# The last branch of a hybrid encoder layer: gate products kept in the gates' tiles, accumulators swapped each chunk, A22 split and multiplied ahead of S4

## The chip, the cores and the metric

The kernel runs on one core of a Trainium2 chip. A core has five instruction streams that work side by side and meet at semaphores: TensorE (PE in the profile; its weight loads are PEld), VectorE (DVE), ScalarE (ACT), GpSimd (POOL) and SyncE (SP, which here only issues DMAs). Each stream executes its own instructions strictly in order. The metric is the device time of one execution in microseconds (us).

## The reference

One layer of an encoder is applied to two requests of 256 and 512 tokens, 768 in all, with the same weights. Cut to the part that the change touches:

```python
h = rmsnorm(x, norm_mix_g)
u, q, k, v, qm, gl = split(h @ w_in)
branches = stack([s5_out, diff_out, mem_out])           # three token mixers
br = einsum('blnc,ncd->blnd', branches, w_branch)       # each projected, 1024 -> 1024
gates = sigmoid(gl + b_gate)
merged = sum(gates * br, axis=branch)
x = x + merged @ w_out                                  # the output projection
h2 = rmsnorm(x, ffn_norm_g)
x = x + (silu(h2 @ w_gate) * (h2 @ w_up)) @ w_down
```

All arrays are float32.

## The kernel before, in words

Activations are kept transposed, features on the 128 partitions and the 768 tokens along the free axis. Every float32 operand of a matmul is held as two parts, hi (`wh`, written by ACT with a copy that rounds) and lo (`wl`, the difference, written by DVE), and a product is three matmuls: hi·hi, hi·lo, lo·hi. They are L755, L756 and L757 of the helper `mm3`, so all products of the kernel carry these three lines, and a profile is read by the tiles.

The branches are projected and merged one after the other: memory attention, S5, and last differential attention. The last one, `branch7`, is what the change touches. It runs in four chunks `c` of 256 output features. In a chunk, the 2x2 blocks of weights (A11 to A22, 512 x 128 each) and of activations (B11 to B22, 512 features x 384 tokens each) are multiplied by the Winograd scheme with seven block products in place of eight: A11·B11, A12·B21, S1·T1, S2·T2, S3·T3, S4·B22 and A22·T4. Each block product is twelve matmuls of 128 x 128 weights on 384 columns. S1 to S4 are sums of weight blocks, made by POOL (L574, L575, L581, L583) in tiles `ws`; S4 overwrites S2. T1 to T4 are sums of activation blocks.

`_split_w` makes a chunk's weights one chunk ahead. `_factor` splits one block into hi and lo (L557 on ACT, L558 on DVE); two blocks share one pair of tiles, so that seven blocks fill three and a half pairs and the last one shares with the next chunk's A11. Raw weights arrive by SP's DMAs in tiles `wr`.

The results of a chunk lie in two accumulator tiles `cs[0]` = (c11, c12) and `cs[1]` = (c21, c22), named `bs` in the profile and taken from a pool of two buffers. Three products (A11·B11, S2·T2, S3·T3) add up in one PSUM bank, `brc`, and are copied out by ACT in between (L1683, L1685, L1690); the others come in banks `br` and are added by DVE (L1673). The gates' logits come from DRAM by a DMA that POOL issues (L1657) into tiles `glr`, of which there are two buffers; ACT makes tanh of them (L1658). `merge(m)` then finishes half m of the chunk, a block M = 2c + m of 128 features: DVE forms (tanh + 1) x accumulator (L1677), the product is added to `merged` (L1678, on POOL for m = 0 and on DVE for m = 1), and `merged` is split into the hi and lo parts of `MG` (L1679 on ACT, L1680 on DVE; tile `mgd`), which are the operand of the output projection.

The output projection (`out_rows`, tiles `wo`) takes the eight blocks M of `MG` as its inner dimension; its weights are w_out, tiles `wr56` to `wr59`, split by L599 (ACT) and L605 (DVE). Its PSUM banks are given out anew when the branch's banks are closed.

A scheduler of the language fixes the order in which each engine's instructions stand, from the order in the code and its own estimate of when each becomes ready. It moves a product ahead of another where it holds it to be ready earlier. In tile names the first number counts the weight matrices in the stream: 52 to 55 are the four chunks of `branch7`, 56 and 57 the first two of w_out. A tile shared by two blocks bears the name of the first (`wl55_S1` holds S1 and S3).

## Time and profile before

| | us |
|---|---|
| three runs | 1741.29, 1742.41, 1743.65 (median 1742.41) |
| the profiled execution, its own time | 1743.06 |
| its span, first to last instruction | 1741.3 |
| PE busy in the span | 1726.6 |
| first matmul of the last branch starts (from the span's start) | 1120.74 |
| first matmul of the output projection starts | 1183.75 |

Times in the trace count from the start of the span. A row of the timeline gives start, duration, engine, line, operation, the tiles written and read, and in brackets how long the engine had been idle and whose work ended that. Durations of matmuls overlap their neighbours, since they are pipelined; the pace of PE is read from one start to the next.

### The profile page before, as it was taken

The numbers are of one execution on the slowest core, as the hardware profiler recorded it, in microseconds if no ns is written. First come the engines' busy times: TensorE is split into PE (matmuls) and PEld (weight loads), VectorE is DVE, ScalarE is ACT, GpSimd is POOL, SyncE is SP. The second block draws the span as 40 slices with busy tenths as digits, with TensorE's granted clock in tenths as the row PEclk, the third lists the DMA queues.
The fourth block names the chain that finished last, engine by engine and source line by source line (L and its number), as shares of the span: only waits on it lengthen the run. The fifth ranks groups of instructions, "written<-read, shape, count | busy, mean of one in ns | idle before, by whom it ended". The sixth has DMA issues, their size and how long they took to land.

```text
span 1741.3 us, 29531 instructions
## 1 busy us (share of the span) xinstructions
PE 1726.6 (99%) x11188; PEld 1608.1 (92%) x11188; DVE 1300.5 (75%) x2405; ACT 908.6 (52%) x1924; POOL 302.5 (17%) x308
## 2 busy tenths in 40 slices
PE   9999999999999999999999999999999999999999
PEld 9999988999999999999989888998889999998887
DVE  7665749699999778887886536685598777776775
ACT  7444543776767346877765434353343333334443
POOL 0000000000000100111000001341036555541130
PEclk9999999999999999999999999999999999999999
DMA  7222636755556454745653435335312323239974
GB/s 268 78 85 91 125 120 135 186 125 143 145 159 159 115 140 103 164 91 156 155 165 117 140 116 157 103 111 174 97 55 91 110 91 109 92 110 295 248 157 97
DMA packets 209213, 234.09 MB, mean 134 GB/s; under 512 B 57832, under 2 KB 173296, under 8 KB 209072
## 3 DMA queue, kind: packets, MB, share of 16 engines
q1 hardware_dynamic: 182160, 167.49, 32.0%
q0 software_dynamic: 17440, 58.34, 15.6%
q10 hardware_dynamic: 9472, 6.39, 1.3%
q8 instruction: 88, 1.44, 0.4%
q14 instruction: 53, 0.43, 0.1%
HBM read 165.78 MB, written 41.22 MB: 119 GB/s over the span
## 4 chain that ended last, share of the span: by engine, by line
PE 95%; DVE 2%; ACT 1%; issue 0%; DMA 0%; POOL 0%; SPq 0%; ACTq 0%; DVEq 0%
PE gl L755 4%; PE gl L756 4%; PE gl L757 4%; PE gate L755 3%; PE gate L756 3%; PE up L756 3%; PE gate L757 3%; PE up L755 3%; PE up L757 3%; PE dn L757 3%; PE dn L755 3%; PE dn L756 3%; PE br L755 3%; PE br L757 3%; PE br L756 3%; PE qk L755 3%
## 5 line engine op out<-in xcount | busy, mean ns | idle before, releaser
L599 ACT ACTIVATE wh<-wr 128x1024 fp32r<-128x1024 f32 x116 | 131.9, 1138 | 52.3 <-PE br L756 13.3
L605 DVE TENSOR_TENSOR wl<-wr,wh 128x1024 fp32r<-128x1024 f32 x74 | 99.2, 1342 | 63.5 <-ACT wh L599 61.7
L755 PE MATMUL gl<-H,wh 128*128 128x256 f32 (+1 forms) x384 | 132.2, 344 | 0.0
L757 PE MATMUL gl<-H,wl 128*128 128x256 f32 (+1 forms) x384 | 129.0, 336 | 0.0
L756 PE MATMUL gl<-H,wh 128*128 128x256 f32 (+1 forms) x384 | 128.7, 335 | 0.0
L603 POOL DMA_DIRECT2D wl<-wr x42 | 36.6, 872 | 483.3 <-ACT wl L602 464.1
L755 PE MATMUL qk<-wh,H 128*128 128x256 f32 x384 | 108.3, 282 | 0.0
L756 PE MATMUL qk<-wl,H 128*128 128x256 f32 x384 | 108.0, 281 | 0.0
L757 PE MATMUL qk<-wh,H 128*128 128x256 f32 x384 | 107.3, 279 | 0.0
L558 DVE TENSOR_TENSOR wl_S<-ws,wh_S 128x512 fp32r<-128x512 f32 x84 | 70.7, 863 | 26.2 <-ACT wh_S L557 26.2
L756 PE MATMUL dn<-wld,dxh 128*128 128x512 f32 x231 | 89.6, 389 | 0.0
L755 PE MATMUL dn<-whd,dxh 128*128 128x512 f32 x231 | 89.5, 389 | 0.0
L757 PE MATMUL dn<-whd,dxl 128*128 128x512 f32 x231 | 88.9, 389 | 0.0
L557 ACT ACTIVATE wh_S<-ws 128x512 fp32r<-128x512 f32 x84 | 49.5, 625 | 73.5 <-PE up L756 36.6
L757 PEld LDWEIGHTS gl<-H,wl 128*128 128x128 f32 x384 | 72.0, 188 | 8.1
L756 PEld LDWEIGHTS gl<-H,wh 128*128 128x128 f32 x384 | 72.2, 188 | 7.2
L755 PEld LDWEIGHTS gl<-H,wh 128*128 128x128 f32 x384 | 72.3, 188 | 6.9
L757 PEld LDWEIGHTS qk<-wh,H 128*128 128x128 f32 x384 | 72.6, 189 | 0.6
L755 PEld LDWEIGHTS qk<-wh,H 128*128 128x128 f32 x384 | 72.4, 188 | 0.6
L756 PEld LDWEIGHTS qk<-wl,H 128*128 128x128 f32 x384 | 72.3, 188 | 0.5
L1296 DVE TENSOR_REDUCE nm<-sc 128x1 f32<-128x512 f32 (+1 forms) x96 | 56.7, 597 | 18.1 <-PE sc L1291 17.2
L1298 ACT ACTIVATE p<-sc,nm 128x512 f32<-128x512 f32 (+1 forms) x96 | 58.8, 615 | 14.4 <-DVE nm L1296 13.9
(535 smaller groups left out, 6076.2 us busy)
## 6 DMA issues: line engine op xcount, KB each, us to landing
wr<-in_w_in_dram SPq DMA_DIRECT2D x48, 512.0 KB, 5.0
wr<-in_w_gate_up_dram SPq DMA_DIRECT2D x44, 512.0 KB, 3.6
wl<-wr POOLq DMA_DIRECT2D x42, 512.0 KB, 5.4
wr<-in_w_branch_dram SPq DMA_DIRECT2D x24, 512.0 KB, 4.5
glr<-gl_scr POOLq DMA_DIRECT2D x24, 384.0 KB, 3.5
hid_scr<-fa SPq DMA_DIRECT2D x11, 768.0 KB, 6.4
wr<-in_w_mem_kv_dram SPq DMA_DIRECT2D x16, 512.0 KB, 4.4
wr<-in_w_in_dram SPq DMA_DIRECT2D x32, 256.0 KB, 3.9
```

What stands on the lines that cost most here:

```text
L557: self.nc.scalar.activation(f(hi), src, AF.Copy)
L558: self.nc.vector.tensor_tensor(out=f(lo), in0=src, in1=f(hi).bitcast(F32), op=ALU.subtract)
L599: self.nc.scalar.activation(hi, r, AF.Copy)
L603: self.nc.gpsimd.dma_start(lo, r.bitcast(F32R), accum_op=ALU.add)
L605: self.sub.tensor_tensor(out=lo, in0=r, in1=hi.bitcast(F32), op=ALU.subtract)
L755: pe.matmul(ps, wh, xh, start=start, stop=False, **kw)
L756: pe.matmul(ps, wh, xl, start=False, stop=False, **kw)
L757: pe.matmul(ps, wl, xh, start=False, stop=stop, **kw)
L1296: v.tensor_reduce(out=nm[:, m : m + 1], in_=ps, axis=AX.X, op=ALU.max, negate=True)
L1298: act.activation(pm[:, 0:n], ps, AF.Exp, bias=nm[:, m : m + 1], accum_out=s1s[:, tt : tt + 1] if m == 0 else s2)
```

## The change

Five things are done, all in the last branch:

- the product of gate and accumulator is written into the gate's tile (`gs[m]`) and no longer into the accumulator, so that an accumulator is free after L1684 (L1677 before), and a gate's tile only after the add to `merged` (L1685);
- in odd chunks the two accumulator tiles change places (`cs.reverse()`);
- in every chunk, and not only in the last, A22·T4 and `merge(1)` stand before S4·B22 and `merge(0)`, and for these weights A22 is split before S4;
- S1·T1 stands before S2·T2;
- in the last chunk the add to `merged` of `merge(0)` is done by DVE, not by POOL.

```diff
-        self._factor(i, "S4", s4)
-        self._factor(i, "A22", A22)
+        for key, src in (("A22", A22), ("S4", s4)) if inplace else (("S4", s4), ("A22", A22)):
+            self._factor(i, key, src)
...
+        def merged_parts(M):
+            act.activation(MG[0][:, M], merged[:, M], AF.Copy, scale=0.5)
+            v.scalar_tensor_tensor(out=MG[1][:, M], in0=merged[:, M], scalar=0.5,
+                                   in1=MG[0][:, M].bitcast(F32), op0=mul, op1=sub)
...
+                if c % 2:
+                    cs.reverse()
...
-                    v.scalar_tensor_tensor(out=cs[m], in0=gs[m], scalar=1.0, in1=cs[m], op0=add, op1=mul)
-                    (v if m else gp).tensor_tensor(out=merged[:, M], in0=merged[:, M], in1=cs[m], op=add)
...
+                    v.scalar_tensor_tensor(out=gs[m], in0=gs[m], scalar=1.0, in1=cs[m], op0=add, op1=mul)
+                    (v if m or c == 3 else gp).tensor_tensor(out=merged[:, M], in0=merged[:, M], in1=gs[m], op=add)
+                    merged_parts(M)
 
                 act.activation(c11, prod("A11", "B11", chain), AF.Copy)
                 plus(c11, prod("A12", "B21"))
-                act.activation(c12, prod("S2", "T2", chain, False), AF.Copy)
                 p5 = prod("S1", "T1")
                 act.activation(c22, p5, AF.Copy)
+                act.activation(c12, prod("S2", "T2", chain, False), AF.Copy)
                 prod("S3", "T3", chain, False)
                 plus(c22, chain)
                 act.activation(c21, chain, AF.Copy)
...
+                plus(c21, prod("A22", "T4"))
+                merge(1)
+                plus(c12, prod("S4", "B22", p5, False))
+                merge(0)
```

What the scheduler makes of it is shown at three places.

**Place 1, the middle of chunk 2.** On PE, before, S1·T1 of chunk 2 (`br_1502`) is followed by the first product of chunk 3 (`brc_1508`), whose third matmul needs the lo part of chunk 3's A11, the second half of `wl54_A22_13775`:

```order
L757 MATMUL br_1502_13972<-rb_12988,wl54_S2_13760 128x384
L755 MATMUL brc_1508_14055<-ra_12987,wh54_A22_13774 128x384 [waits Activation_49]
L756 MATMUL brc_1508_14055<-ra_12987,wh54_A22_13774 128x384
L757 MATMUL brc_1508_14055<-ra_12987,wl54_A22_13775 128x384 [waits DVE_49]
L755 MATMUL brc_1508_14055<-ra_12987,wh54_A22_13774 128x384
```

Now only the two matmuls with the hi part stand there:

```order
L757 MATMUL br_1502_13959<-rb_12988,wl54_S2_13760 128x384
L755 MATMUL brc_1508_14055<-ra_12987,wh54_S4_13774 128x384 [waits Activation_49]
L756 MATMUL brc_1508_14055<-ra_12987,wh54_S4_13774 128x384
L755 MATMUL brc_1500_13931<-rc_12989,wh54_S2_13759 128x384 [waits Activation_49]
L756 MATMUL brc_1500_13931<-rc_12989,wh54_S2_13759 128x384
```

The first matmul with the lo part has moved behind 36 others: S2·T2, A22·T4 and S4·B22 of chunk 2. Three more of that product follow, and then S3·T3 of chunk 2, which waits for the copy of c12 out of the bank on ACT. That copy, with its neighbours on ACT, before:

```order
L1679 ACTIVATE mgd_13595<-merged_11575 128x768 [waits DVE_49]
L1687 ACTIVATE bs_1499_13930<-br_1502_13972 128x384 [waits PE_49]
L1658 ACTIVATE glr_1497_13926<-glr_1497_13926 128x768 [waits DMASW3_49,Activation_49]
L557 ACTIVATE wh55_S1_13906<-ws550_13896 128x512 [waits PE_49,Activation_49]
L1685 ACTIVATE bs_1498_13929<-brc_1500_13931 128x384 [waits PE_49]
```

and now:

```order
L1649 ACTIVATE mgd_13595<-merged_11575 128x768 [waits DVE_49]
L557 ACTIVATE wh55_S1_13906<-ws550_13896 128x512 [waits PE_49,Activation_49]
L1692 ACTIVATE bs_1498_13929<-brc_1500_13931 128x384 [waits PE_49]
L1663 ACTIVATE glr_1497_13926<-glr_1497_13926 128x768 [waits DMASW3_49,Activation_49]
L557 ACTIVATE wh55_S1_13906<-ws552_13910 128x512 [waits Pool_49]
```

The copy (L1685, now L1692) stands behind the hi part of block M = 3 of `merged` in both, and the tanh of the gate has gone behind it.

**Place 2, the end of chunk 2 on DVE.** The rows begin with the add to c22, and the gate's tile `glr_1497` is freed for the last gate (`glr_1505`) by L1677 before:

```order
L1673 TENSOR_TENSOR bs_1499_13930<-bs_1499_13930,brc_1500_13931 128x384 [waits PE_49]
L605 TENSOR_TENSOR wl56_0_14036<-wr56_0_13778,wh56_0_14035 128x1024 [waits DMAHW5_49,Activation_49]
L1673 TENSOR_TENSOR bs_1499_13930<-bs_1499_13930,br_1503_14017 128x384 [waits Activation_49]
L1680 SCALAR_TENSOR_TENSOR mgd_13595<-merged_11575,mgd_13595 128x768 [waits Activation_49]
L1673 TENSOR_TENSOR bs_1506_14053<-bs_1506_14053,br_1509_14069 128x384 [waits DVE_49,PE_49,Activation_49]
L1677 SCALAR_TENSOR_TENSOR bs_1499_13930<-glr_1497_13926,bs_1499_13930 128x768 [waits DVE_49]
```

and by L1685 now:

```order
L1680 TENSOR_TENSOR bs_1499_13930<-bs_1499_13930,brc_1500_13931 128x384 [waits PE_49]
L558 TENSOR_TENSOR wl55_A22_13916<-wr55_1_13747,wh55_A22_13915 128x512 [waits Activation_49]
L558 TENSOR_TENSOR wl55_A22_13916<-ws551_13897,wh55_A22_13915 128x512 [waits Activation_49]
L1680 TENSOR_TENSOR bs_1499_13930<-bs_1499_13930,br_1503_14000 128x384 [waits Activation_49]
L1684 SCALAR_TENSOR_TENSOR glr_1497_13926<-glr_1497_13926,bs_1499_13930 128x768 [waits DVE_49]
L605 TENSOR_TENSOR wl56_0_14036<-wr56_0_13778,wh56_0_14035 128x1024 [waits DMAHW5_49,PE_49,Activation_49]
L1680 TENSOR_TENSOR bs_1507_14054<-bs_1507_14054,br_1509_14069 128x384 [waits PE_49,Activation_49]
L1685 TENSOR_TENSOR merged_11575<-merged_11575,glr_1497_13926 128x768 [waits DVE_49]
```

The splits of A22 and S4 of chunk 3, which stood ahead of these rows, now stand among them.

**Place 3, from the branch to the output projection.** On PE the last block product was S4·B22 (`br_1510`):

```order
L757 MATMUL br_1510_14096<-rb_12988,wl55_S4_13916 128x384
L755 MATMUL br_1510_14096<-rb_12988,wh55_S4_13915 128x384
L756 MATMUL br_1510_14096<-rb_12988,wh55_S4_13915 128x384
L757 MATMUL br_1510_14096<-rb_12988,wl55_S4_13916 128x384
L755 MATMUL wo_1514_14205<-wh56_0_14035,mgd_13595 128x512 [waits Activation_49]
```

It is S3·T3 now (`brc_1508`), with S4·B22 directly before it:

```order
L757 MATMUL brc_1508_14055<-rc_12989,wl55_S1_13907 128x384
L755 MATMUL brc_1508_14055<-rc_12989,wh55_S1_13906 128x384
L756 MATMUL brc_1508_14055<-rc_12989,wh55_S1_13906 128x384
L757 MATMUL brc_1508_14055<-rc_12989,wl55_S1_13907 128x384
L755 MATMUL wo_1514_14205<-wh56_0_14035,mgd_13595 128x512 [waits Activation_49]
```

In both, the first matmul of the output projection (`wo_1514`) waits for ACT's last copy out of `brc_1508` (L1690, now L1695). On ACT before:

```order
L1658 ACTIVATE glr_1505_14050<-glr_1505_14050 128x768 [waits DMASW5_49,Activation_49]
L599 ACTIVATE wh57_0_14193<-wr57_0_13921 128x1024 [waits DMAHW7_49,PE_49,Activation_49]
L1690 ACTIVATE bs_1507_14054<-brc_1508_14055 128x384 [waits DVE_49]
L599 ACTIVATE wh57_1_14199<-wr57_1_14039 128x1024 [waits DMAHW0_49,PE_49]
L1679 ACTIVATE mgd_13595<-merged_11575 128x768 [waits DVE_49]
```

and now:

```order
L1663 ACTIVATE glr_1505_14050<-glr_1505_14050 128x768 [waits DMASW5_49]
L599 ACTIVATE wh57_0_14193<-wr57_0_13921 128x1024 [waits DMAHW7_49,PE_49,Activation_49]
L599 ACTIVATE wh57_1_14199<-wr57_1_14039 128x1024 [waits DMAHW0_49,PE_49]
L1649 ACTIVATE mgd_13595<-merged_11575 128x768 [waits DVE_49]
L1695 ACTIVATE bs_1506_14053<-brc_1508_14055 128x384 [waits DVE_49]
```

The copy now stands behind the hi part of block M = 6 (L1649), which waits for DVE's add to `merged` (L1685); on DVE that add stands directly behind the lo part of `wr57_0` (L605), which waits for ACT's L599 of the same tile.

13 lines of the change are left out of this document (removed).

## The prediction

> **What bounds the kernel now.** I read the page's chain of work first, then TensorE's timeline through the last branch, then the other engines' timelines at the places where TensorE stops. The page:
>
> ```profile
> span 1741.3 us, 29531 instructions
> ...
> PE 95%; DVE 2%; ACT 1%; issue 0%; DMA 0%; POOL 0%; SPq 0%; ACTq 0%; DVEq 0%
> ...
> wr<-in_w_branch_dram SPq DMA_DIRECT2D x24, 512.0 KB, 4.5
> ```
>
> TensorE is the chain nearly everywhere, so a change is worth what it takes from, or adds to, the time in which TensorE does not start matmuls. TensorE's timeline in the last branch, from its first matmul to the first of the output projection:
>
> ```profile
> 1120.74 0.34 PE L755 MATMUL brc<-ra,wh_A 128*128 128x384 f32 x1
> ...
> 1154.03 0.33 PE L755 MATMUL br<-rb,wh_S 128*128 128x384 f32 x1
> ...
> 1156.28 0.34 PE L756 MATMUL brc<-ra,wh_A 128*128 128x384 f32 x1
> 1158.74 0.44 PE L757 MATMUL brc<-ra,wl_A 128*128 128x384 f32 x1 [2.12 <-DVE wl_A L558]
> ...
> 1159.89 0.49 PE L757 MATMUL brc<-ra,wl_A 128*128 128x384 f32 x1
> ...
> 1163.36 0.34 PE L756 MATMUL brc<-rc,wh_S 128*128 128x384 f32 x1
> ...
> 1175.12 0.45 PE L755 MATMUL brc<-rc,wh_A 128*128 128x384 f32 x1 [0.33 <-ACT bs L1683]
> ...
> 1181.50 0.33 PE L757 MATMUL brc<-rc,wl_S 128*128 128x384 f32 x1
> ...
> 1183.75 0.39 PE L755 MATMUL wo<-wh,mgd 128*128 128x512 f32 x1
> ```
>
> From 1154.03 to 1156.28 are 13 starts, 0.173 us each. The branch has 28 products of 12 matmuls, 336 x 0.173 = 58.1 us; it takes 1183.75 - 1120.74 = 63.0. So 4.9 us are lost, 0.28% of the time, and no rearrangement of the branch can gain more. Most of it hangs on one place: TensorE stands at 1156.28 (2.46 - 0.17 = 2.3 us) for the lo part of chunk 3's A11, and from 1159.89 to 1163.36 eleven matmuls take 3.47 us in place of 1.90, 1.6 us more. The windows view tells why (columns: stretch, length, busy time of PE, PEld, DVE, ACT, POOL, granted clock, DMA):
>
> ```profile
> 1160.00:1163.00 3.00, 3.00 (x11) 3.00 (x10) 3.00 (x5) 1.30 (x2) 0.55 (x1) 0.50 0.44 150
> 1175.00:1179.00 4.00, 3.88 (x22) 3.88 (x23) 3.53 (x5) 1.83 (x4) 0.54 (x1) 1.00 0.73 229
> ```
>
> After the long stop the clock is 0.50; after the stop of 0.33 us at 1175 it stays 1.00.
>
> Why was the lo part late? VectorE and GpSimd:
>
> ```profile
> 1155.15 3.54 DVE L558 TENSOR_TENSOR wl_A<-wr,wh_A 128x512 fp32r<-128x512 f32 x2
> 1158.61 0.54 DVE L1673 TENSOR_TENSOR bs<-bs,br 128x384 f32<-128x384 f32 x1
> ...
> 1169.75 0.68 DVE L558 TENSOR_TENSOR wl_S<-ws,wh_S 128x512 fp32r<-128x512 f32 x1
> ```
>
> ```profile
> 1154.24 2.22 POOL L1678 TENSOR_TENSOR merged<-merged,bs 128x768 f32<-128x768 f32 x1 [2.34 <-DVE bs L1677]
> 1156.42 1.71 POOL L574 TENSOR_TENSOR ws<-wr,wr 128x512 f32<-128x512 f32 x1
> 1158.08 0.55 POOL L1657 DMA_DIRECT2D glr<-gl_scr  x1
> ```
>
> Two splits that take 0.68 each elsewhere took 3.54 while GpSimd ran its add and its sum. A VectorE operation on two SBUF tiles stands still while GpSimd works on SBUF. This work of the two engines together is nearly as long as TensorE's, and the change leaves it almost as it was, so I follow VectorE, not TensorE, through the changed order.
>
> **The change part by part.** The durations I use, from VectorE and ScalarE:
>
> ```profile
> 1161.31 0.94 DVE L1680 SCALAR_TENSOR_TENSOR mgd<-merged,mgd 128x768 fp32r<-128x768 f32 x1
> 1162.18 0.54 DVE L1673 TENSOR_TENSOR bs<-bs,br 128x384 f32<-128x384 f32 x1
> 1162.65 0.94 DVE L1678 TENSOR_TENSOR merged<-merged,bs 128x768 f32<-128x768 f32 x1
> ...
> 1170.93 0.96 DVE L1677 SCALAR_TENSOR_TENSOR bs<-glr,bs 128x768 f32<-128x768 f32 x1
> 1172.22 0.56 DVE L1673 TENSOR_TENSOR bs<-bs,brc 128x384 f32<-128x384 f32 x1 [0.33 <-PE brc L757]
> ...
> 1176.62 0.94 DVE L1677 SCALAR_TENSOR_TENSOR bs<-glr,bs 128x768 f32<-128x768 f32 x1
> ...
> 1181.94 0.56 DVE L1673 TENSOR_TENSOR bs<-bs,brc 128x384 f32<-128x384 f32 x1 [0.78 <-PE brc L757]
> 1183.10 1.23 DVE L605 TENSOR_TENSOR wl<-wr,wh 128x1024 fp32r<-128x1024 f32 x1 [0.60 <-ACT wh L599]
> 1184.24 1.01 DVE L1673 TENSOR_TENSOR bs<-bs,br 128x384 f32<-128x384 f32 x2
> ...
> 1188.05 0.95 DVE L1678 TENSOR_TENSOR merged<-merged,bs 128x768 f32<-128x768 f32 x1
> ```
>
> ```profile
> 1162.33 0.84 ACT L1658 ACTIVATE glr<-glr 128x768 f32<-128x768 f32 x1 [1.70 <-DMA glr<-gl_scr]
> ...
> 1173.85 0.85 ACT L1679 ACTIVATE mgd<-merged 128x768 fp32r<-128x768 f32 x1 [0.36 <-POOL merged L1678]
> 1174.60 0.47 ACT L1683 ACTIVATE bs<-brc 128x384 f32<-128x384 f32 x1
> ...
> 1181.28 0.85 ACT L1658 ACTIVATE glr<-glr 128x768 f32<-128x768 f32 x1 [0.75 <-DMA glr<-gl_scr]
> 1182.03 1.04 ACT L599 ACTIVATE wh<-wr 128x1024 fp32r<-128x1024 f32 x1
> 1182.98 0.47 ACT L1690 ACTIVATE bs<-brc 128x384 f32<-128x384 f32 x1
> ...
> 1189.03 0.85 ACT L1679 ACTIVATE mgd<-merged 128x768 fp32r<-128x768 f32 x1 [4.19 <-DVE merged L1678]
> ```
>
> ```profile
> 1171.97 1.84 POOL L1678 TENSOR_TENSOR merged<-merged,bs 128x768 f32<-128x768 f32 x1 [3.29 <-DVE bs L1677]
> ...
> 1177.87 0.54 POOL L1657 DMA_DIRECT2D glr<-gl_scr  x1 [3.54 <-DVE bs L1677]
> ```
>
> From start to start a 384-column add costs VectorE 0.47 (1162.18 to 1162.65), a 768-column operation 0.87 (1161.31 to 1162.18), a 1024-column split 1.14 (1183.10 to 1184.24). I start at 1158.61, the add to c21 of chunk 1, which in both orders follows the two slow splits. (That the engines get there at the same time is a choice: up to place 1 both orders have the same work and TensorE loses almost nothing.)
>
> *Place 1: the stop of 2.3 us and its half clock go.* The first matmul with the late lo part now comes 36 matmuls, 6.2 us, later than 1156.45, at 1162.7, and the part is there at 1158.7. So 3.9 us are won here, for the moment. Next late is S3·T3 of chunk 2, which needs the copy of c12 (L1692). TensorE gets there after 12 + 2 + 36 + 3 = 53 matmuls: 1154.03 + 9.2 = 1163.2. The copy stands behind the hi part of M = 3, which waits for VectorE: 1158.61 + 0.47 (c21) + 0.87 (L1684) + 0.87 (L1650) + 0.47 (c11) + 0.68 (split) = 1161.97, where the add to `merged` (L1685) starts. The hi part starts 0.98 after such an add (1188.05 to 1189.03), 1162.95; 0.75 later (1173.85 to 1174.60) a split, for which I take 0.6, near VectorE's 0.68 for the same columns; the copy then takes 0.52 until TensorE goes on (1174.60 to 1175.12): 1164.8. A new stop of 1.6 us, between nothing, if VectorE is that much earlier, and the 2.3 that it replaces.
>
> *Gates kept in the gates' tiles.* A gate's tile is now freed by the add, one VectorE operation later than by L1677, and the load is on POOL's queue behind that. First for the second gate of chunk 2: add ends 1162.9, load issued 0.3 later (1176.62 + 0.94 to 1177.87), tanh 3.41 after the issue (1177.87 to 1181.28): 1166.6. S3's hi part stands behind that tanh: 1166.6 + 0.75 + 0.6 = 1168.0, its lo part 1168.7, the add to c12 1169.2, L1684 to 1170.1, where the add to c22 starts: 2.1 us before the 1172.22 of now. VectorE keeps about half of what place 1 won.
>
> *Place 2 gives most of the rest back.* POOL's add starts 1.04 after L1684 starts (1170.93 to 1171.97), 1170.2, and holds SBUF for 1.84, so that the splits of A22 and S4, now behind the add to c22, run from 1172.1 to 1173.4. Then c21 to 1173.9, L1684 to 1174.8, L605 to 1175.9, c11 to 1176.4, L1685 to 1177.3. The load of the last gate is issued at 1177.6, and its tanh starts at 1181.0, against 1181.28 now. On the way TensorE stops again: A22·T4 of chunk 3 takes the bank that c21's add frees at 1173.9, and TensorE gets there 43 matmuls after 1164.8, at 1172.2, so it waits 1.7. Its last product, 91 matmuls after 1164.8, ends at 1164.8 + 15.7 + 1.7 = 1182.2.
>
> *Place 3 is what decides.* Now the bank of the output projection's first matmul is freed by L1690 at 1182.98, while S4·B22 covers it: 12 matmuls from 1181.50 on, 2.1 us. In the changed order S3·T3 is last, so this cover is gone, and the copy stands behind the last tanh, two L599, and the hi part of M = 6 with VectorE's L605 and add before it. From the tanh: 0.75 to L599 (1181.28 to 1182.03), 1.07 to L605 (to 1183.10), 1.14 to the add, 0.98 to the hi part, 0.75 to the copy, 0.52 to TensorE, together 5.2. TensorE goes on at 1186.2 in place of 1183.75: **+2.5 us**, after standing for 4.0. The low end is +1.5 (everything on VectorE 1 us earlier, as far as it is ahead at place 1 with no stop there), the high end +4.6 (the 2.1 us are not kept). I take the sum as it is.
>
> *The half clock after that stop.* It is longer than the 2.12 that was followed by 3.47 us at 0.50, so I add the measured **1.6 us**; the low end is 0, what the stop of 0.33 cost.
>
> The Trainium skill, "TensorE: Matmul & The Clock Gate", section "Part 1: The HAM clock gate (the "warmup" mystery)", says that the clock is either full or half, and that this is decided by a free-running window of about 3.4 us. The trace agrees with its 0.50 for 3.47 us. By that rule a stop of 4 us can fall so that two windows are too idle, and the sum would be 5.7 in place of 4.1, a rival below.
>
> *Edits that I cost at nothing.* Swapped accumulators and the earlier copy of c11 end the wait of 0.33 at 1175.12, but VectorE is later there, which hides it. S1·T1 before S2·T2 changes ScalarE's order only. SP's load of the third w_out tile waits for A22's split, now at 1172.7, and L599 wants it at 1181.7; a load of that size lands in 4.5 (the page's row). POOL's last add of 1.84 goes to VectorE for 0.95; it is the add of the chain above, counted there. The gaps after it are covered: the second half of the inner dimension needs M = 7 only after 24 matmuls of the output projection. The output projection and all behind it is the same, so a late start shifts the end.
>
> Sum: 2.5 + 1.6 = +4.1 us on the profiled execution's own 1743.06, which lies 0.65 above the median of the runs, 1742.41. Against the median: **1746.5 us**, 0.24% slower.
>
> **The rivals.**
>
> - The clock stays full after the stop: +2.5, 1744.9. For it: where the windows fall is chance. Against: a shorter stop brought 0.50.
> - Two slow stretches: 1742.4 + 2.5 + 2 x 1.6 = 1748.1, with the stop at both sides of a window as its condition; only one such stretch is in this trace.
> - VectorE is not ahead at the end of chunk 2: the add to c22 starts at 1172.2, the last gate comes 2.1 later, 1748.6. For it: the load issued at 1158.08 took 4.25 until its tanh at 1162.33, not 3.41, and two loads are in my chain.
> - The other side: the output projection isn't held by the last gate. Then its start is the end of S3·T3 plus 0.44 (1181.50 to 1181.94), 0.56 and 0.52, 1.5 us; with no new stops S3·T3 ends at 1120.74 + 58.1 = 1178.9, the projection starts at 1180.4, 3.4 early: 1739.0. It decides if the last tanh starts before about 1175.4, nearly 6 us before my sum; with the new stops it gives 1742.3, no change.
>
> That the code's order isn't the program's is seen at place 3: the code puts S4·B22 last, the scheduler S3·T3. I count with the program's.
>
> **How the numbers follow.** My sum 0.48 (1745.5 to 1747.7), clock full 0.22, two slow stretches 0.10, VectorE late 0.10, the other side 0.10. 0.2%, 3.5 us, is about what a measurement of this kernel can tell from no change. Slower by more, above 1745.9: three quarters of the first and the two long ones, 0.56. Faster by more, below 1738.9: half of the last, 0.05. The rest, 0.39, is within. The range 1742.0 to 1749.0 leaves out most of the last rival and the tails of the long ones.
>
> **What would show it.** Right: no stop at the first product of chunk 3; TensorE waiting about 1.6 us for ScalarE's copy before S3·T3 of chunk 2; the first `wo` matmul waiting about 4 us for L1695 and a clock of 0.50 after it; the last tanh near 1181. Wrong: the first `wo` with less than 2 us of wait, or the last tanh before 1179, which would mean that VectorE and GpSimd were not the bound in chunk 3.

## The result

The changed kernel takes 1747.18 us (median of 11 runs, 1744.74 to 1748.84); the kernel before, beside it, 1742.41 (11 runs, 1741.03 to 1743.65). The ratio is 1.0027, with a 95% interval of 1.0017 to 1.0036: slower, by about as much as was forecast (1746.5). The profiled execution of the changed kernel is its fastest: 1744.74, with a span of 1743.0. A second profiled execution of the same kernel (`again`, below) took 1745.96. The two together show more than either, so both stand here. One further run of that second set took 3638.91 us, twice the others, and is left out of its numbers.

TensorE's timeline in the last branch, changed kernel, first execution (start, duration, and in brackets how long it was idle before and what ended that):

```profile
1119.79 0.34 PE L755 MATMUL brc<-ra,wh_A 128*128 128x384 f32 x1
...
1162.76 0.44 PE L755 MATMUL brc<-rc,wh_S 128*128 128x384 f32 x1 [0.33 <-ACT bs L1692]
...
1172.33 0.44 PE L755 MATMUL br<-mgd,wh_A 128*128 128x384 f32 x1 [1.84 <-DVE bs L1680]
...
1182.16 0.34 PE L757 MATMUL brc<-rc,wl_S 128*128 128x384 f32 x1
1185.38 0.50 PE L755 MATMUL wo<-wh,mgd 128*128 128x512 f32 x1 [2.88 <-ACT bs L1695]
```

and in the second:

```profile
1119.40 0.34 PE L755 MATMUL brc<-ra,wh_A 128*128 128x384 f32 x1
...
1180.28 0.34 PE L757 MATMUL brc<-rc,wl_S 128*128 128x384 f32 x1
1184.95 0.74 PE L755 MATMUL wo<-wh,mgd 128*128 128x512 f32 x1 [4.33 <-ACT bs L1695]
```

The stop within chunk 3's first product is gone. TensorE stands instead for 0.5 us before S3·T3 of chunk 2, for 2.0 before A22·T4 of chunk 3 (1170.15 to 1172.33 less one matmul of 0.17), and, after S3·T3 as its last product, for 3.05 (first execution) or 4.50 (second) until ScalarE has copied c21 out of the bank.

The executions differ in where the branch starts (1118.7 to 1121.2 us over all the profiles of this study), so the measure from here on is **the branch's length**, from its first matmul to the first `wo` matmul, and **the tail**, from there to the end. The windows view gives both (columns as in the prediction). Before:

```profile
1120.74:1183.75 63.01, 60.56 (x337) 59.72 (x336) 51.49 (x62) 33.86 (x59) 26.93 (x22) 0.97 0.38 119
1183.75:1741.30 557.55, 552.68 (x2902) 509.83 (x2901) 402.57 (x564) 214.12 (x342) 197.43 (x149) 1.00 0.46 132
```

After, first execution, with the slow stretch in the middle of the branch:

```profile
1119.79:1185.38 65.59, 60.53 (x338) 59.57 (x336) 54.23 (x65) 36.34 (x60) 29.18 (x27) 0.97 0.38 118
1185.38:1743.00 557.62, 552.77 (x2901) 509.96 (x2901) 398.92 (x561) 212.29 (x340) 193.12 (x144) 1.00 0.45 131
...
1173.30:1176.80 3.50, 3.50 (x13) 3.50 (x13) 3.46 (x5) 2.06 (x3) 0.54 (x1) 0.51 0.75 277
```

After, second execution, with the slow stretch behind the first `wo` matmul:

```profile
1119.40:1184.95 65.55, 58.99 (x337) 58.03 (x335) 53.81 (x64) 36.02 (x60) 29.37 (x28) 1.00 0.41 128
1184.95:1744.20 559.25, 554.42 (x2901) 511.12 (x2901) 398.91 (x561) 212.43 (x340) 192.60 (x142) 1.00 0.46 130
...
1184.95:1188.45 3.50, 3.50 (x8) 2.76 (x9) 3.43 (x5) 0.00 (x0) 0.00 (x0) 0.51 0.98 368
```

So the branch is 2.58 and 2.54 us longer, in both. In the first execution 3.50 us at a clock of 0.51 lie inside the branch, behind the stop of 2.0, and cost nothing: the last product ends 1.5 us later against the branch's start (62.54 against 61.05), but the `wo` matmul comes at the same place, since it waits for ScalarE and not for TensorE. In the second execution the same slow stretch lies behind the seam (the change from the branch to the output projection), where nothing waits for anything but TensorE, and the tail is 559.25 in place of 557.55 to 557.62: +1.65. For these two executions that is the whole account: +2.55 in both, and +1.6 when the slow stretch falls behind the seam.

Two things stand beside it. The spans of the first execution and of the kernel before differ by only 1.70 us, since its branch also started 0.95 earlier (1119.79 against 1120.74), for a reason that was not looked for. And the 63.01 of the kernel before hold a slow stretch of their own, 1.6 us that no later wait absorbs. Against an execution of it without that stretch the changed branch would be some 4.1 us longer; this is an estimate from the 1.6, and `vector_adds_before` below, with a stop nearly as long and no slow stretch, has 61.19.

The chain at the seam, changed kernel, first execution. Columns: start, duration, engine, line, operation, tiles; in brackets the idle time before and what ended it. ScalarE:

```profile
1179.91 0.85 ACT L1663 ACTIVATE glr<-glr 128x768 f32<-128x768 f32 x1 [1.45 <-DMA glr<-gl_scr]
...
1184.11 0.84 ACT L1649 ACTIVATE mgd<-merged 128x768 fp32r<-128x768 f32 x1 [0.69 <-DVE merged L1685]
1184.86 0.47 ACT L1695 ACTIVATE bs<-brc 128x384 f32<-128x384 f32 x1
```

and VectorE:

```profile
1181.99 1.22 DVE L605 TENSOR_TENSOR wl<-wr,wh 128x1024 fp32r<-128x1024 f32 x1
1183.12 0.95 DVE L1685 TENSOR_TENSOR merged<-merged,glr 128x768 f32<-128x768 f32 x1
1183.99 0.55 DVE L1680 TENSOR_TENSOR bs<-bs,brc 128x384 f32<-128x384 f32 x1
```

From the last tanh to the first `wo` matmul are 5.47 us (1179.91 to 1185.38). The copy L1695 stands directly behind the hi part; the add to c22, which has to be done before it too, ends 0.3 us ahead of it.

### The profile page after: what moved, and what is told of

It is laid out like the page before. It is cut to its first block, busy times and chain, and to the rows that moved or that the text cites. A ratio compares the mean times of both kernels' runs of the same rounds, so it can differ in the third digit from the quotient of the medians.

```text
span 1743.0 us, 29532 instructions
## 1 busy us (share of the span) xinstructions
PE 1725.7 (99%) x11188; PEld 1607.4 (92%) x11188; DVE 1301.1 (75%) x2406; ACT 909.6 (52%) x1924; POOL 299.3 (17%) x307
## 4 chain that ended last, share of the span: by engine, by line
PE 95%; DVE 2%; ACT 1%; issue 1%; DMA 1%; POOL 0%; SPq 0%; ACTq 0%; DVEq 0%
PE gl L755 4%; PE gl L757 4%; PE gl L756 4%; PE gate L755 3%; PE gate L756 3%; PE gate L757 3%; PE up L756 3%; PE up L755 3%; PE up L757 3%; PE dn L757 3%; PE dn L755 3%; PE dn L756 3%; PE br L755 3%; PE br L757 3%; PE br L756 3%; PE qk L755 3%
## 5 line engine op out<-in xcount | busy, mean ns | idle before, releaser
L599 ACT ACTIVATE wh<-wr 128x1024 fp32r<-128x1024 f32 x116 | 131.9, 1138 | 51.1 <-PE br L756 12.9
L605 DVE TENSOR_TENSOR wl<-wr,wh 128x1024 fp32r<-128x1024 f32 x74 | 98.7, 1335 | 62.5 <-ACT wh L599 60.8
L558 DVE TENSOR_TENSOR wl_S<-ws,wh_S 128x512 fp32r<-128x512 f32 x82 | 68.8, 860 | 24.9 <-ACT wh_S L557 24.8
```

What stands on the lines that cost most here:

```text
L558: self.nc.vector.tensor_tensor(out=f(lo), in0=src, in1=f(hi).bitcast(F32), op=ALU.subtract)
L599: self.nc.scalar.activation(hi, r, AF.Copy)
L605: self.sub.tensor_tensor(out=lo, in0=r, in1=hi.bitcast(F32), op=ALU.subtract)
```

## Experiments

Each was run with the kernel before on the same chip; its median there was 1742.32, 1742.51, 1741.89 and 1741.97 us in the four groups. The ratios are not the plain quotients of the medians, but lie within 0.0004 of them. A table first, with the branch's length and the tail of each profiled execution:

| run | edit | length | tail | median | ratio to before, 95% interval |
|---|---|---|---|---|---|
| before | | 63.01 | 557.55 | 1742.41 | |
| changed | | 65.59 | 557.62 | 1747.18 | 1.0027, 1.0017 to 1.0036 |
| again | changed, unaltered | 65.55 | 559.25 | 1746.22 | 1.0019, 1.0010 to 1.0028 |
| seam_pinned | changed, cover and copy put right | 63.54 | 557.57 | 1742.70 | 0.9999, 0.9991 to 1.0008 |
| pins_only | changed, copy put right | 64.77 | 557.65 | 1743.88 | 1.0012, 1.0003 to 1.0021 |
| add_on_gpsimd | changed, last add back on GpSimd | 64.68 | 559.19 | 1745.42 | 1.0014, 1.0006 to 1.0023 |
| s3t3_last | before, two products swapped | 65.54 | 557.66 | 1744.76 | 1.0014, 1.0005 to 1.0023 |
| gates_only | before, gate products in gates' tiles | 66.87 | 559.15 | 1747.19 | 1.0025, 1.0015 to 1.0036 |
| a22_only | before, A22 first | 66.40 | 559.26 | 1746.22 | 1.0021, 1.0012 to 1.0031 |
| all_but_gates | changed, without that part | 67.80 | 559.17 | 1748.00 | 1.0036, 1.0022 to 1.0049 |
| filled_stop | changed, 18 matmuls more | 64.25 | 557.53 | 1744.41 | 1.0011, 1.0002 to 1.0020 |
| vector_adds | changed, no adds on GpSimd | 62.91 | 559.96 | 1744.14 | 1.0014, 1.0005 to 1.0023 |
| vector_adds_before | before, no adds on GpSimd | 61.19 | 557.65 | 1740.26 | 0.9988, 0.9979 to 0.9997 |
| seam_and_vector | seam_pinned, no adds on GpSimd | 59.92 | 557.51 | 1740.34 | 0.9989, 0.9980 to 0.9998 |

Every tail is one of three: 557.5 to 557.7, 559.15 to 559.26 (with one slow stretch behind the seam), and once 559.96.

### The changed kernel a second time

> The changed kernel unaltered, for a second profiled execution and for how far the runs spread. My account: the median is 1747.2 +/- 1.0, the stops in the branch stand where they stood (0.5 us before S3*T3 of chunk 2, about 2.0 before A22*T4 of chunk 3, about 3.0 before the first wo matmul, which starts 64.6 us after the branch's first), and a run is longer by about 1.6 us for each 0.001 that its mean clock is lower, since each stretch of half clock costs that much. Rival: the spread of the runs has nothing to do with the clock, and the stops themselves differ by more than 0.5 us between the two executions.

Measured: median 1746.22; stops of 0.55, 2.02 and 4.50; length 65.55. The first two stops and the length are as expected, the third stop differs by 1.45 us, and the rival is right to that extent: it is longer because S3·T3 ended earlier, with no slow stretch ahead of it. The first `wo` matmul stands where it stood. The runs at a mean clock of 0.999 took 1744.14 to 1746.86, those at 0.998 took 1746.05 to 1746.96; in the first set of runs, 1744.74 and 1744.83 at 0.999 against 1746.25 to 1748.84 at 0.997. So in the first set the time follows the clock, and in the second hardly: from 0.999 to 0.998 the medians differ by 0.3 us and not by the expected 1.6. That a stretch inside the branch costs nothing would explain it; the runs without a profile do not show where their stretches lay.

### Is it the seam?

Last chunk alone: S4·B22 is issued behind S3·T3's last matmul, and the add to `merged` of M = 6 and its parts behind the add to c22 and the copy of c21.

```diff
-                plus(c22, chain)
-                act.activation(c21, chain, AF.Copy)
+                s3 = last[0]                       # S3*T3's last matmul
+                r22 = plus(c22, chain)
+                r21 = act.activation(c21, chain, AF.Copy)
                 plus(c21, prod("A22", "T4"))
                 merge(1)
-                plus(c12, prod("S4", "B22", p5, False))
-                merge(0)
+                with tc.issue_after(s3.ins) if c == 3 else ExitStack():
+                    q5 = prod("S4", "B22", p5, False)
+                plus(c12, q5)
+                merge(0, (r22, r21) if c == 3 else None)
```

> Last chunk alone: TensorE issues S4*B22 behind S3*T3, and ScalarE's copy of c21 and VectorE's add to c22 are issued ahead of the add to merged and the parts of M = 6. My account (the wait for that copy is what the output projection waits for, and S4*B22 is its cover): S3*T3 ends at 1180.4 on the time axis of the changed kernel's trace, copy and add end by 1181.2, S4*B22 covers them, the first wo matmul starts at 1182.4 to 1183 without a stop over 0.5; the parts of M = 6 and 7 then come at 1188 to 1189, up to 1.5 us later than the second half of the projection's inner dimension wants them. Median 1.5 to 3 us below the changed kernel's: 1744.2 to 1745.7. Rival (the loss is at the stop before A22*T4 of chunk 3 or spread over the branch): median within 0.7 us of the changed kernel's 1747.2.

The seam's rows in this run, TensorE and ScalarE (L1700 is the copy of c21 here):

```profile
1183.93 0.39 PE L755 MATMUL wo<-wh,mgd 128*128 128x512 f32 x1
```

```profile
1182.99 0.47 ACT L1700 ACTIVATE bs<-brc 128x384 f32<-128x384 f32 x1
```

The first `wo` matmul waits for nothing: S4·B22 covers the copy. The branch is 2.05 us shorter than the changed kernel's, the median 1742.70, 3.5 to 4.5 below it and level with the kernel before. The first `wo` matmul was expected 62.6 to 63.2 us after the branch's first and came at 63.54 (with a slow stretch, and 1.0 us of stop before S3·T3 of chunk 2). The median fell by more than expected, which would fit a seam without a stop that a slow stretch could follow, though no run isolates that; and the parts of M = 6 and 7 were not late, as I had feared: no matmul of the output projection waited. The rival does not hold: the loss is at the seam.

The same without the order on TensorE (`issue_after(s3.ins)` left out):

> The run seam_pinned without its order on TensorE: the copy of c21 and the add to c22 are issued ahead of the add to merged of M = 6 and its parts, but S3*T3 stays TensorE's last product, without S4*B22 as a cover. My account (the queue in front of the copy and the missing cover each cost a part): first wo 64.0 to 64.8 us after the branch's first matmul (changed 65.6, seam_pinned 63.5), after a stop of 2 to 3.8 us, so that the half clock stays a matter of chance; median 1744.3 to 1746.0, between the two. Rival 1 (the cover does nothing): first wo at 63.5 +/- 0.3, median at seam_pinned's 1742.7 +/- 0.7. Rival 2 (the pins do nothing): first wo at 65.4 to 65.8, median 1746.3 to 1747.5.

Measured: length 64.77 and median 1743.88, 0.4 below the expected range; the stop is 2.05, and 4.10 us lie between the last tanh (1180.15) and

```profile
1184.25 0.50 PE L755 MATMUL wo<-wh,mgd 128*128 128x512 f32 x1 [1.88 <-ACT bs L1698]
```

Of the 2.05 us by which `seam_pinned` is shorter than the changed kernel, 0.8 come with this edit and 1.2 with the order on TensorE. Neither rival holds. The 1.2 are not the cover alone: here the add to c22 stands behind the split L605 and the copy behind a second L599, in `seam_pinned` both stand ahead of them. Both executions also have a slow stretch inside the branch; `seam_pinned` pays it in full, while here the stop absorbs it. The split holds for these two executions only.

Next, the smallest edit of the change, the add of M = 6 in the last chunk:

```diff
-                    (v if m or c == 3 else gp).tensor_tensor(out=merged[:, M], in0=merged[:, M], in1=gs[m], op=add)
+                    (v if m else gp).tensor_tensor(out=merged[:, M], in0=merged[:, M], in1=gs[m], op=add)
```

> The last add to merged of M = 6 goes back to GpSimd; everything else is as in the changed kernel. The order then has the copy of c21 directly behind the two L599, ahead of the hi part of M = 6. My account (this small edit, which I costed as a part of the chain, is what put the copy behind the hi part): the copy starts at about 1183.3 in place of 1184.86, VectorE's add to c22 at 1183.1 to 1184.2 according to how long GpSimd's add holds the split before it; first wo at 1183.9 to 1185.0 in place of 1185.38, median 0.4 to 1.5 us below the changed kernel's. Rival (the last gate's tanh sets the seam, whatever stands behind it): first wo at 1185.4 +/- 0.2 and the median unchanged; or, with GpSimd's add holding VectorE back, later by up to 1 us.

Measured: the copy at 1183.47, the first `wo` at 1184.01, length 64.68 (0.9 less), median 1745.42 (0.8 below the changed kernel's in the same group, 1.8 below its first set). With the add on GpSimd the scheduler puts the copy ahead of the hi part, as expected. VectorE, seam, this run:

```profile
1181.20 1.77 DVE L605 TENSOR_TENSOR wl<-wr,wh 128x1024 fp32r<-128x1024 f32 x1 [1.21 <-ACT wh L599]
1182.89 0.54 DVE L1680 TENSOR_TENSOR bs<-bs,brc 128x384 f32<-128x384 f32 x1
```

GpSimd's add holds the split L605 for half a microsecond (1.77 in place of 1.22), and the copy waits for the add to c22 behind it. The profiled stop of 3.76 is followed by a slow stretch (tail 559.19).

### What the cover is worth in the kernel before

TensorE's last two products change places, everything else is the kernel before:

```diff
-                prod("S3", "T3", chain, False)
+                if c == 3:
+                    prod("S4", "B22", p5, False)
+                with tc.issue_after(last[0].ins) if c == 3 else ExitStack():
+                    prod("S3", "T3", chain, False)
...
-                    plus(c12, prod("S4", "B22", p5, False))
+                    plus(c12, p5)
```

> The kernel before, with TensorE's last two products of the branch changing places in chunk 3: S4*B22 first, S3*T3 last. VectorE's add to c22 then stands behind the split L605, and the copy of c21 behind both L599, as the scheduler places them. My account, formed after the single-part runs, which all had S3*T3 last and all lost (this order of 24 matmuls is by itself the loss at the seam): from the last tanh 4.5 to 5.0 us to the first wo, as in the runs gates_only and a22_only, so first wo 64.5 to 65.5 us after the branch's first matmul (before: 63.0), after a stop of 1.5 to 2.5 us; median 1744.0 to 1746.0. Rival (a late last gate is needed too; with the early one of the kernel before the copy comes in time): first wo 63.0 to 63.8, median 1742 to 1743.3.

```profile
1185.74 0.50 PE L755 MATMUL wo<-wh,mgd 128*128 128x512 f32 x1 [1.68 <-ACT bs L1694]
```

Measured: length 65.54, a stop of 1.85, median 1744.76, and 5.20 us from the last tanh to the first `wo`: the account holds, with length and chain just above their ranges, and the rival does not. 24 matmuls in another order, and the order of the copies that the scheduler makes of it, cost 2.5 us of length, as much as the whole change. Not all of the 2.5 is the seam's stop; a second stop of 0.97 us, before the product now in the place of S3·T3 (0.80 of it idle, for ScalarE's copy out of S1·T1's bank), came with the swap.

### Which part of the change brings that order?

One part alone, and all but one part. Gate products in the gates' tiles, alone:

```diff
-                    v.scalar_tensor_tensor(out=cs[m], in0=gs[m], scalar=1.0, in1=cs[m], op0=add, op1=mul)
-                    (v if m else gp).tensor_tensor(out=merged[:, M], in0=merged[:, M], in1=cs[m], op=add)
+                    v.scalar_tensor_tensor(out=gs[m], in0=gs[m], scalar=1.0, in1=cs[m], op0=add, op1=mul)
+                    (v if m else gp).tensor_tensor(out=merged[:, M], in0=merged[:, M], in1=gs[m], op=add)
```

> The kernel before, with the gate products kept in the gates' tiles and nothing else. In the order S3*T3 is already TensorE's last product of the branch, and S3*T3's copy stands behind the last tanh and two L599. My account (cover gone, copy behind a late tanh; the tile freed one operation later): first wo 64.0 to 65.5 us after the branch's first matmul (before: 63.0), median 1743.5 to 1746. Rival 1 (the order of A22 and S4 makes the loss): median within 0.7 us of 1742.4 and first wo at 63.0 +/- 0.4. Rival 2 (the part brings a gain that the others spoil): below 1741.7.

Measured: length 66.87, median 1747.19, above both expected ranges and as slow as the whole change. The last tanh is at 1182.09 and

```profile
1186.55 0.50 PE L755 MATMUL wo<-wh,mgd 128*128 128x512 f32 x1 [4.06 <-ACT bs L1690]
```

4.46 us later. That tanh is at 62.4 us after the branch's first matmul, 2.3 later than in the changed kernel. Here the stop of the kernel before ahead of chunk 3 is left too (1.77 us).

A22 split and multiplied first, alone (in every chunk):

```diff
-        self._factor(i, "S4", s4)
-        self._factor(i, "A22", A22)
+        for key, src in (("A22", A22), ("S4", s4)) if inplace else (("S4", s4), ("A22", A22)):
+            self._factor(i, key, src)
...
-                if c < 3:
+                if False:
```

> The kernel before, with A22 split ahead of S4 and A22*T4 multiplied ahead of S4*B22 in every chunk, and nothing else. S3*T3 is TensorE's last product here too, with the copy of c21 directly behind the two L599, but the last gate's load is issued behind L677's operation, some 2.5 us earlier against the branch than in the changed kernel. My account (it takes both: the cover gone and the late gate): the last tanh starts 57 to 58.5 us after the branch's first matmul, first wo at 62.3 to 63.5 after it (before 63.0, changed 65.6), median 1741.5 to 1743.5. Rival (S3*T3 as the last product is enough): first wo at 64.5 to 65.5, median 1744.5 to 1746.5.

And the changed kernel with the gate products back in the accumulators' tiles (the first diff of this part, reversed, in the changed kernel):

> The changed kernel, with the gate products written to the accumulators' tiles again, so that a gate's tile is freed by that product and not by the add behind it. My account (the gate's late load sets the seam): the last tanh starts 57 to 58.5 us after the branch's first matmul, in place of 60.1; first wo 62.5 to 64.0 after it, median 1742 to 1744.5. Rival (any of the orders with S3*T3 last costs as much): first wo at 65 +/- 0.5, median within 1 us of 1747.

The waits of TensorE in the branch (engine, tile, line, what it waited for: us in all, times, longest), first of `a22_only`, then of `all_but_gates`:

```profile
PE br L755 <- DVE bs L1673: 2.6, 1, 2.6
PE brc L757 <- DVE wl_S L558: 2.0, 1, 2.0
PE wo L755 <- ACT bs L1690: 1.7, 1, 1.7
PE br L755 <- ACT bs L1687: 0.7, 1, 0.7
```

```profile
PE wo L755 <- ACT bs L1695: 2.9, 1, 2.9
PE br L755 <- DVE bs L1680: 2.5, 1, 2.5
PE brc L757 <- DVE wl_S L558: 2.0, 1, 2.0
```

My account fell in both: lengths of 66.40 and 67.80 where I had 62.3 to 64.0, medians 1746.22 and 1748.00. The last gate's load was issued no earlier than in the changed kernel (56.2 and 56.1 us after the branch's first matmul, there 56.2), and the tanh was later still: in both, TensorE waits 2.0 us for the lo part of chunk 3's A11 (in these orders it lies in the tile named after S4), the stop of the kernel before, and 2.5 to 2.6 for the add to c21 that frees A22·T4's bank; the tanh stands on ScalarE behind a hi part that waits 3.52 us for VectorE's add to `merged` (tanh at 1182.60 and 1181.18, 61.4 and 62.0 us after the branch's first matmul, against 60.1 in the changed kernel). The parts don't add up: alone they cost 3.7 (A22) and 4.9 us (gates), together with the rest 3.9 to 4.8, and the change without its gate part 5.5. What the four have in common is S3·T3 as the last product. `s3t3_last` shows that this order costs 2.5 us of length; that it is the common cause is the reading that fits all of them, not something one run isolates in each.

### Does a stop cost more than its own length?

The changed kernel with 18 matmuls added behind S3·T3 in the last chunk, A22·T4 repeated into its own bank; it computes the same:

```diff
-                plus(c21, prod("A22", "T4"))
+                p7 = prod("A22", "T4")
+                if c == 3:
+                    with tc.issue_after(s3.ins):
+                        prod("A22", "T4", p7, ks=range(2))
+                        prod("A22", "T4", p7)
+                plus(c21, p7)
```

> The changed kernel with work added: in the last chunk TensorE repeats A22*T4 one and a half times (18 matmuls, 3.1 us, into the same bank, the last full pass giving the same product) behind S3*T3, where it stood for 3.0 to 4.5 us. In this order the copy of c21 goes ahead of the hi part of M = 6, which brings the first wo forward by up to 1 us. My account (a stop of over 2 us is followed by half clock, and a slow stretch behind the seam costs 1.6 us in full): no half clock behind the seam, first wo 64.3 to 66.0 after the branch's first matmul, median 1 to 2.5 us below the changed kernel's. Rival (the chip pays for idle TensorE nothing beyond the idle time): median unchanged within 0.7 us, or longer by up to 3.1 if the added matmuls lie in the path.

Windows of this run, the branch and the tail:

```profile
1119.12:1183.37 64.25, 62.14 (x356) 61.28 (x355) 53.36 (x64) 35.31 (x59) 29.30 (x28) 1.00 0.38 122
1183.37:1740.90 557.53, 552.70 (x2902) 509.86 (x2901) 399.32 (x561) 213.34 (x342) 192.68 (x143) 1.00 0.45 131
```

3.1 us of work more, and the median is 1.8 to 2.8 us lower (1744.41). The length fell by 1.3, more than expected and for the reason given ahead of the run: the scheduler put the copy ahead of the hi part. The rest, 0.5 to 1.5 us, I put down to slow stretches behind the seam that the runs no longer pay: three of the eleven runs have a mean clock of 1.000 (1741.95 to 1742.65), which none of the changed kernel's 22 has. Since the order moved too, and a slow stretch ahead of the seam is no longer absorbed by a stop there, the fill's own share is not shown.

### GpSimd's adds

In the changed kernel, in the kernel before, and in `seam_pinned`, the adds to `merged` of the last branch that GpSimd does go to VectorE (`v.tensor_tensor` in place of `(v if m else gp).tensor_tensor`).

> The changed kernel with GpSimd's three remaining adds to merged moved to VectorE; S3*T3 stays TensorE's last product and the copy of c21 stays behind the hi part of M = 6. My account (two separate causes; this takes away VectorE's waiting for GpSimd only): no stop before A22*T4 of chunk 3, all splits L558 of the branch under 0.8 us, first wo 62 to 64.5 us after the branch's first matmul in place of 65.6, with a stop of 2 to 5 us left before it; median 1742 to 1745.5. Rival (the whole of the gain of the run seam_and_vector comes from the two together, because the seam eats whatever TensorE wins ahead of it): first wo at 65.0 to 66.0, median 1746 to 1748.

```profile
1183.74 0.79 PE L755 MATMUL wo<-wh,mgd 128*128 128x512 f32 x1 [4.50 <-ACT bs L1695]
```

```profile
1181.00:1182.00 1.00, 0.00 (x0) 0.00 (x0) 1.00 (x2) 0.26 (x1) 1.00 (x3) 1.00 0.53 115
1182.00:1183.00 1.00, 0.00 (x0) 0.00 (x0) 1.00 (x3) 0.53 (x1) 0.69 (x2) 0.51 0.99 397
...
1183.74:1188.80 5.06, 5.06 (x12) 4.00 (x13) 4.08 (x6) 0.84 (x1) 0.00 (x0) 0.50 0.99 383
...
1183.74:1743.70 559.96, 555.18 (x2901) 511.66 (x2901) 398.63 (x561) 212.18 (x340) 192.21 (x142) 0.99 0.45 130
```

No stop is left ahead of the seam: TensorE has done the branch in 58.2 us and then stands for 4.66. The length is 62.91, a hair under the kernel before, and yet this execution took 1745.51 (the median is 1744.14): half clock for 5.06 us behind the stop makes the tail 2.4 us longer. The clock is already at 0.51 in the last part of the stop, from 1182.0 on, so that the stretch lasts 6.8 us in all, and 1.7 of them cost nothing.

The account holds in length, stop and median, and the rival does not: the last product ends 2.8 to 4.3 us earlier against the branch's start than in the two executions of the changed kernel, and the first `wo` comes 2.65 earlier, since the last tanh is earlier too (57.7 us after the first matmul, 60.1 in the changed kernel). One part of it failed: two splits L558 of 1.78 us are left, beside GpSimd's sums, though no stop comes of them.

> The kernel before with GpSimd's adds to merged in the last branch moved to VectorE, one word in one line. My account (the stop of 2.3 us and its half clock came from two splits that stood beside GpSimd's add and sum, and S4*B22 still covers the seam): the two splits ahead of chunk 3 take 1.4 to 2.2 us in place of 3.54, the stop is under 0.8 us with no half clock, first wo 59.5 to 61.5 us after the branch's first matmul (before: 63.0), median 1739.5 to 1741.5. Rival (VectorE's own work becomes the bound, or GpSimd's sums L574 to L583 hold it as much as the adds did): first wo 62.5 to 64.5, median 1742 to 1744.5.

VectorE ahead of chunk 3, and the matmul that waits for it:

```profile
1154.13 2.35 DVE L558 TENSOR_TENSOR wl_A<-wr,wh_A 128x512 fp32r<-128x512 f32 x2
```

```profile
1156.54 0.44 PE L757 MATMUL brc<-ra,wl_A 128*128 128x384 f32 x1 [2.00 <-DVE wl_A L558]
```

Length and median as expected (61.19 and 1740.26), the reason only in part: the two splits take 2.35 in place of 3.54, still 1.1 more than the 1.29 of two others at 1150.95, and the stop is still 2.17 us long, with GpSimd's sum L575 (1153.47, 1.86 us) beside the first. In this execution no slow stretch followed it; 1.8 us of length have gone, of which 1.6 is the half clock. The clock is not the whole gain of the median: among the runs at a mean clock of 1.000 the kernel before took 1740.50 to 1742.22 (8 runs), this one 1739.24 to 1740.51 (6 runs). Where the rest of it lies stays open, since the profile shows only 0.2 us of length beside the half clock.

> The kernel of the run seam_pinned, with the three adds to merged that GpSimd still does moved to VectorE. My account (GpSimd's add holds VectorE back for longer than the add itself takes there: the split beside it takes 2.09 us in place of 0.68, the add 0.87 on VectorE): the split of A22 in chunk 3 takes 0.68, the stop before A22*T4 of chunk 3 shrinks from 2.0 us to 0.5 to 1.3, first wo 62.0 to 63.3 us after the branch's first matmul (seam_pinned: 63.5), median 1740.5 to 1742.5, the first that is below the kernel before. Rival (VectorE is full; the added 2.6 us make everything behind it later, the gates' loads too): stop of 2 us or more, first wo at 63.5 to 65.5, median 1743 to 1746.

```profile
1165.44 0.69 DVE L558 TENSOR_TENSOR wl_A<-wr,wh_A 128x512 fp32r<-128x512 f32 x1 [0.16 <-ACT wh_A L557]
...
1166.51 0.69 DVE L558 TENSOR_TENSOR wl_A<-ws,wh_A 128x512 fp32r<-128x512 f32 x1
```

The splits take 0.69, the stop before A22·T4 is gone altogether, and one of 1.56 us before S3·T3 in the last chunk is what is left. The branch takes 59.92 us, 1.8 more than its matmuls alone and 2.1 less than the account's lowest; median 1740.34. This kernel and `vector_adds_before` are the two that beat both kernels, by about 0.1% against the kernel before, with intervals that just leave out no change.

## Why the prediction was right

By its steps, each against the branch's first matmul where the two executions differ in their start.

- **Place 1.** Right that the stop and its half clock go. The new stop at S3·T3 of chunk 2, which the prediction gave as a sign of being right, was mis-sized: 0.50 to 0.55 us, not 1.6. The step that failed is the choice that both orders reach the add to c21 of chunk 1 at the same time. VectorE, changed kernel:

```profile
1152.46 1.87 DVE L558 TENSOR_TENSOR wl_S<-ws,wh_S 128x512 fp32r<-128x512 f32 x1
1154.25 1.78 DVE L558 TENSOR_TENSOR wl_S<-wr,wh_S 128x512 fp32r<-128x512 f32 x1
1155.95 0.54 DVE L1680 TENSOR_TENSOR bs<-bs,br 128x384 f32<-128x384 f32 x1
...
1168.65 0.55 DVE L1680 TENSOR_TENSOR bs<-bs,brc 128x384 f32<-128x384 f32 x1
1169.12 2.09 DVE L558 TENSOR_TENSOR wl_A<-wr,wh_A 128x512 fp32r<-128x512 f32 x1
1171.14 0.68 DVE L558 TENSOR_TENSOR wl_A<-ws,wh_A 128x512 fp32r<-128x512 f32 x1
1171.74 0.54 DVE L1680 TENSOR_TENSOR bs<-bs,br 128x384 f32<-128x384 f32 x1
```

  That add is at 36.2 us after the branch's start (1155.95 - 1119.79), in the kernel before at 37.9: 1.7 us earlier. The two splits still take 3.65 us beside GpSimd; they only start earlier.
- **Gates' tiles.** The add to c22 of chunk 2 at 48.9 against a forecast of 49.4 (1170.1 - 1120.74): VectorE's 1.7 us had shrunk to 0.5 by there. The path was another than the forecast one, which had S3's hi part behind the second gate's tanh. The tanh ends in time, and ScalarE then stands for GpSimd's sum:

```profile
1165.92 0.63 ACT L557 ACTIVATE wh_S<-ws 128x512 fp32r<-128x512 f32 x1 [0.55 <-POOL ws L581]
```

  That sum had waited 1.51 us for a split on VectorE, which stood behind an L1650 of 2.07 us (0.94 elsewhere) beside GpSimd's sum L583.
- **Place 2.** Right. The split of A22 took 2.09 us behind GpSimd's add, the stop before A22·T4 of chunk 3 was 2.0 (forecast 1.7), the last tanh at 60.1 (forecast 60.3). What the sum did not have is that this stop too can be followed by half clock, as in the first execution; it came to nothing, since the seam absorbs it.
- **Place 3.** The path is right: the first `wo` waits for the copy L1695, and the chain from the last gate's load leads to it. That the size is right to a tenth (+2.58 and +2.54 us of length against +2.5) is in part luck, since errors cancel: the last gate's load was issued 0.6 us earlier than forecast (56.25 us after the branch's first matmul against 56.86), its tanh came 3.87 us after that and not 3.41 (4.01 in the second execution), and the chain behind the tanh took 5.47 (5.23) and not 5.2. The stop is 3.05 or 4.50, around the forecast of 4.0. `seam_pinned` takes the loss away, `pins_only` about two fifths of it, and `s3t3_last` makes one of the same size in the kernel before.
- **The half clock behind the seam.** The forecast of 1.6 us is the 1.65 of the second execution. The first execution is the rival with full clock, forecast 1744.9, measured 1744.74; so close is luck, since its branch started 0.95 us earlier than in the profile that the sum started from. `vector_adds` shows the condition of the rival with two stretches, 6.8 us at half clock, of which 5.06 fell on matmuls, for 2.4 more in the tail. The Trainium skill ("TensorE: Matmul & The Clock Gate", section "Part 1: The HAM clock gate") speaks of free-running windows of about 3.4 us, one of which must be busy before full speed returns; the traces agree with 3.40 to 3.42 us for a stretch and 6.82 for the long one.
- **Edits costed at nothing.** The last add, which went to VectorE and which I counted only as a step of the chain, also moved the copy of c21 behind the hi part: 0.9 us of length (`add_on_gpsimd`). The swap of the accumulators and the order of S1·T1 and S2·T2 were not tried apart.
- **The other side**, with the output projection not held by the last gate and no new stops, was to start `wo` 59.7 us after the branch's first matmul, for 1739.0. `seam_and_vector` starts it at 59.92, with a median of 1740.34 (its profiled execution, the fastest, took 1738.59). The price of the branch was right; it takes two more edits to get there, with the last tanh at 57.5 and the copy ahead of the hi part.
- **The median** lies 0.7 above the forecast, and in the second set of runs 0.3 below it. That is closer than the sum deserves. It has one slow stretch, and the median run of the first set has a mean clock of 0.997, which by the lengths above is two to three of them (an estimate). No profile shows where they lay; those of other runs have stretches also at 907 to 912 us (`seam_pinned`, `pins_only`, `a22_only`) and at 11 to 15 (`a22_only`, `vector_adds`), far ahead of the branch.

What stays open: why the scheduler makes S3·T3 the last product as soon as either main part of the change is in. The orders show that it does; its costs were not looked into. Open too is how much of the loss is the missing cover and how much the order of the copies, which no run separates cleanly.

## What to carry over

Where one stage hands its PSUM bank to the next, look at what TensorE does while the bank is being emptied: a product that needs no part of that bank covers the wait, and a change of order anywhere upstream can lose it; here the orders with and without it differ by 2.5 us in the kernel before, copies included. Time that TensorE alone loses ahead of such a wait is free (1.5 us of half clock in the first execution); what moves the wait is the chain that ends it. Measure to the first instruction behind the wait, not to the stops. And when VectorE's work is on the path, try its partner's long adds on VectorE itself before looking for a better order: one word gained about 0.1% here, which a rearrangement of the whole branch did not.

## What the runs showed of the hardware

- **A stop of 2 us may or may not halve the clock.** Over the 14 profiled executions here, stops of TensorE in the branch and at its end of 1.5 to 2.8 us were followed by half clock in 7 cases of 18 (2.0 in the first execution of the changed kernel, but not 2.02 in the second, nor 2.79 in `a22_only`); stops above 3 us in 5 of 6 (not the 3.05 of the changed kernel's first execution). In the pair of executions of one kernel nothing else differs, so it isn't the program alone that decides.
- **A slow stretch had the same length each time**: in windows of 1 us over the 14 executions the time at half clock comes to 3.40 to 3.42 us in each of 16 stretches (the last 3 us of the kernel left out), and where all of it falls on matmuls that wait for nothing it costs 1.6 to 1.7 us. After the longest stop of all (4.66) it was 6.82 us, twice that; 1.7 of them lay in the stop itself, and the rest cost 2.4.
- **More work can take less time**: 18 added matmuls in a stop, with a median 1.8 to 2.8 us lower, 1.3 of it with another order of the copy.
- **GpSimd's operations lengthen VectorE's with two SBUF inputs that run beside them**: a split of 0.68 us took 2.09 beside an add of 1.85, one of 1.22 took 1.77 to 2.38. Beside a sum (1.86) two splits took 2.35 in place of 1.29. An add with one input in PSUM kept its 0.54 (L1680 at 1151.99 in the changed kernel, beside GpSimd's add of 2.23).
